# A two-layer decoder trunk: SwiGLU before the weight splits, first units split inside the down loop, transposes behind half a tile, another first chunk

## The chip, the cores and the metric

One core of a Trainium2 chip. The metric is device time in microseconds (us), the median of the runs of the whole program.

## The reference

Two post-norm layers on x of 512 tokens by 1024 features, float32. Each layer has three sub-layers; each sees x scaled and shifted by vectors made from a conditioning vector c.

```python
cond = jax.nn.silu(c)
for l in range(DEPTH):                       # DEPTH = 2
    mod = cond @ w_ada[l] + b_ada[l]         # nine vectors of 1024
    sh1, sc1, g1, sh2, sc2, g2, sh3, sc3, g3 = jnp.split(mod, 9)
    y = _swiglu(x * (1 + sc1) + sh1, ...)    # (silu(h @ w_gate) * (h @ w_up)) @ w_down, D_FF = 2816
    x = layer_norm(ALPHA * x + 0.5 * (1 + g1) * y)
    y = _token_mixer(x * (1 + sc2) + sh2, w_in[l], w_out[l])
    x = layer_norm(ALPHA * x + (1 + g2) * y)
    y = _swiglu(x * (1 + sc3) + sh3, ...)
    x = layer_norm(ALPHA * x + 0.5 * (1 + g3) * y)
```

The token mixer (retention, dilated and stick-breaking heads between two projections) is not touched.

## The kernel before

**Products.** Every weight product is done in three matmuls (`mm3`, L181 to L183): both operands are split into a rounded part `hi` and a remainder `lo`, and hi x hi, hi x lo and lo x hi are added in PSUM. A *unit* is a 128 x 1024 piece of a weight matrix. `unit` (L167) loads it into one of three `raw` buffers, ScalarE casts it to `hi` (L176) and VectorE takes the difference `lo` (L177). `hi` and `lo` go to one of four buffers of their own, or, for a unit marked spare, to two of the 22 large buffers that also hold the hidden tiles. All loads are issued by SyncE in one queue.

**Background.** The modulation vectors of later sub-layers are made meanwhile from 512 KB pieces of w_ada, which pass through the same three `raw` buffers: a load and a multiply-add on VectorE (L205) for each of eight pieces, then a reduction across partitions on GpSimd (L209) and a few operations on VectorE (L216 to L221). `pacer` (L264) spreads these steps evenly over a number of calls. A multiply-add is issued one step after its load.

**A feed-forward** (`ffn`, L445). The 22 hidden tiles (128 features by 512 tokens) come in groups of two, one group last where the number is odd, as in the first feed-forward, where three tiles are made in the start-up. A group takes four units (two for a single tile): gate, then up. When the gate products are done, ScalarE takes silu (L415); when the up products are done, VectorE multiplies (L420), ScalarE casts (L421) and VectorE takes the difference (L422). After each unit the unit four places on is loaded and split (`load(1)`) and the background advances (`next(pace)`). Then the down product: for each of the first 18 hidden tiles i one unit of w_down serves four row tiles of 128 tokens with two PSUM banks each, all eight; it is 24 matmuls (`rows_mm`, L397 to L401). The last four units are kept for a tail that goes row tile by row tile (`rows_tail`), so that the norm of one runs under the products of the next. Between loop and tail, `prefetch()` loads and splits the first four units of the next sub-layer.

**Between two sub-layers** (`PostNorm`, L317). For each row tile: gate, residual and statistics on VectorE (L349 to L354), the root on GpSimd (L146), the scaling on ScalarE (L362). `make_h` transposes normalised tiles for the next sub-layer: 16 transposes for a pair of row tiles (L297), scale and shift on ScalarE and VectorE (L301, L303), cast and difference (L307, L308). The first pair is done in `head()`, after the products of row tile 2 and before those of row tile 3; the second pair in `rest()`, inside the next sub-layer.

**The start-up** (`startup`, L1041) makes the first sub-layer's modulated x in eight chunks of 128 features. `sums(k)` loads the chunk's shift and scale weights and x, multiplies by c on VectorE and GpSimd and adds; `chunk(k)` finishes the sum with a matmul against ones (L1092), transposes x (L1089), and makes `hT_hi` and `hT_lo`; then the three hidden tiles get the chunk's products.

The order on each engine is set by a scheduler from the order of the program and its own estimates of time; `issue_after(ins)` puts what follows behind `ins` on the same engine's queue, without a wait of its own.

Of the kernel before, what the change touches and what calls it, by code (L numbers as in the profile page):

```python
# [67 lines left out]
def trunk(ctx: ExitStack, tc: tile.TileContext, x_in, c_in, w_ada, b_ada, ln_gain, ln_bias,  # L68
# [47 lines left out]
    def load_cols():  # L116
        pt = psum()
        for l in range(DEPTH):
            PE.transpose(out=pt[:, l * NB:(l + 1) * NB], in_=brows[:, l, :], identity=ident[0:NB, 0:NB])
        V.tensor_copy(out=bcol.rearrange("p l c -> p (l c)"), in_=pt[:, 0:DEPTH * NB])  # L120
# [166 lines left out]

    def make_h(pair, h, a, b):
        hh, hl = h
        sl = slice(pair * 256, pair * 256 + 256)  # L290
        for k2 in range(KC // 2):
            ps = psum()
            tmp = work([P, 512], "htmp")
            for i in range(2):
                k = k2 * 2 + i
                for t in range(2):
                    PE.transpose(out=ps[:, i * 256 + t * P:i * 256 + (t + 1) * P],  # L297
                                 in_=xres[pair * 2 + t][:, k * P:(k + 1) * P], identity=ident)
# [18 lines left out]
    class PostNorm:  # L317
# [58 lines left out]

        def head(self):

            if self.h is not None:
                make_h(0, self.h, self.a, self.b)  # L380

# [21 lines left out]
    def rows_part(ps, parts, cs, fresh):  # L403
        for i, ((sh, sl), (wh, wl)) in enumerate(parts):
            mm3(ps, sh, sl, wh[:, cs], wl[:, cs], fresh and i == 0, i == len(parts) - 1)
        return ps
# [6 lines left out]
    def silu(ps_g):  # L413
        sg = work([P, T], "sg")
        S.activation(out=sg, in_=ps_g, func=AF.Silu)  # L415
        return sg

    def glu(sg, ps_u):
        g = big([P, 2, T], F32R, "gT")
        V.tensor_tensor(out=sg, in0=sg, in1=ps_u, op=ALU.mult)  # L420
        S.copy(out=g[:, 0, :], in_=sg)  # L421
# [13 lines left out]
    REST_AT_Q = 3  # L435
    AHEAD = 3
    RES, RES_END = 4, 8
    ACT_HEADS = (1, 3)
# [6 lines left out]
    def ffn(l, s, wg, wu, wd, h, pre, gt, rest, prefetch, nxt):  # L445
# [56 lines left out]
        for i in range(NF - res):  # L502
# [24 lines left out]

    def proj_units(l, off, spare=False):
        return [unit(w_in[l, kh * 512:(kh + 1) * 512, off:off + 256].rearrange("(k p) f -> p k f", p=P), (4, 256), spare)
                for kh in range(2)]  # L530

# [27 lines left out]
    def mixer(l, h, pre, rest, prefetch, nxt):  # L559
# [469 lines left out]
        for k in range(4):  # L1029
            ws(k)  # L1030
        npre = prefetch()
        pn = PostNorm(l, 1, nxt)
# [8 lines left out]
    def startup():  # L1041
# [6 lines left out]
        def sums(k):  # L1048
# [27 lines left out]
            last = V.tensor_tensor(out=accs[0], in0=accs[0], in1=accs[1], op=ALU.add)  # L1076
            with tc.issue_after(last.ins), tc.issue_after(cond_ins.ins):
                uls[k] = unit([(0, f1g[0, cs, 0:384]), (1, f1u[0, cs, 0:384])], (2, 384))
            return accs[0], last

        def chunk(k, acc):
            cs = slice(k * P, (k + 1) * P)
            if k == 0:
                load_cols()
                V.tensor_copy(out=bc0[:, 0, :], in_=mod_bias(0, 0))
                V.tensor_scalar(out=bc0[:, 1, :], in0=mod_bias(0, 1), scalar1=1.0, scalar2=None, op0=ALU.add)
            px = psum()
            for t in range(NT):
                PE.transpose(out=px[:, t * P:(t + 1) * P], in_=xres[t][:, cs], identity=ident)  # L1089
            pc = psum()  # L1090
            for m in range(2):
                PE.matmul(pc[:, m:m + 1], lhsT=acc[:, m, :], rhs=ones[:, 0:1], start=True, stop=True)  # L1092
            ab0 = small([P, 2], "ab0")
            V.tensor_tensor(out=ab0, in0=pc[:, 0:2], in1=bc0[:, :, k], op=ALU.add)
            tmp = work([P, T], "htmp")
            S.activation(out=tmp, in_=px, func=AF.Identity, scale=ab0[:, 1:2], bias=ab0[:, 0:1])
            S.copy(out=hh[:, k, :], in_=tmp)  # L1097
            done = V.tensor_tensor(out=hl[:, k, :], in0=tmp, in1=hh[:, k, :].bitcast(F32), op=ALU.subtract)  # L1098
            return done

        acc, last = sums(0)
        last = chunk(0, acc)
# [15 lines left out]
        load_cols2()  # L1118
        return h, [glu(silu(pss[0][m]), pss[1][m]) for m in range(3)]

# [11 lines left out]
    def first_units(l, s):  # L1132
        if l >= depth:
            return None
        if s == 1:
            return proj_units(l, OFF["sv"], True) + proj_units(l, OFF["sq"], True)
        return [u() for u in gu_loads(l, *((f1g, f1u) if s == 0 else (f2g, f2u)), 0, 2, True)]

# [43 lines left out]
```

## Time and profile before

| | |
|---|---|
| runs | 1986.51 us median of 3 (1985.47 to 1992.09) |
| the profiled execution | 1992.88 us, of which span 1991.1 |
| mean granted TensorE clock | 0.995 |
| TensorE busy with matmuls | 1951.0 us, 98% |
| VectorE, ScalarE, GpSimd busy | 1146.7, 685.3, 234.3 us |
| moved by DMA | 263.12 MB |

The first feed-forward runs from the start to 405 us, the first mixer to about 640, then two feed-forwards with a boundary at 1011.5, the second mixer from 1380, and the last feed-forward to the end. Matmuls overlap, so a TensorE that is busy to 98% isn't at its peak; what counts are the stretches in which it stands still or has a low clock. In a row of an engine's order, the brackets hold how long the engine sat idle before the instruction, and what ended that.

### The profile page before, as it was taken

The page shows a single profiled execution, that of the slowest core. Times are in us where ns is not written, and L with a number is a line of the kernel's source. Part 1 is how long each engine was busy: PE and PEld are TensorE (multiplying, and loading weights), DVE is VectorE, ACT ScalarE, POOL GpSimd, SP SyncE. Part 2 cuts the span into 40 slices and gives each one's busy share as a digit, 9 for nine tenths or more (in the row PEclk, how much of TensorE's full clock was granted, in tenths as well). Part 3 has the DMA queues.
Part 4 walks back from the last instruction along what each step waited for, and adds up shares of the span by engine and source line. Part 5 has one row for each costly group of instructions (what it writes and reads, how often), then busy time and mean ns, then how long its engine had stood idle before and what let it go on. Part 6 is the DMA issues. An engine that isn't in the chain of part 4 may idle for free.

```text
span 1991.1 us, 24802 instructions
## 1 busy us (share of the span) xinstructions
PE 1951.0 (98%) x10008; PEld 1637.6 (82%) x10008; DVE 1146.7 (58%) x1525; ACT 685.3 (34%) x952; POOL 234.3 (12%) x180
## 2 busy tenths in 40 slices
PE   7999979999999999999999999999999999999998
PEld 5888868898888988888888888888887888888887
DVE  8555664556767575664567455436576665434327
ACT  3322221346653323231242233213575442222220
POOL 5011111103210011110101011010133000001000
PEclk9999989999999999999999999999999999999999
DMA  9555555532222445545424444442322223434231
GB/s 291 165 172 177 182 170 166 169 106 80 75 73 75 136 160 172 177 159 177 141 92 156 155 158 159 148 148 85 106 69 83 75 74 106 128 125 138 96 106 53
DMA packets 177930, 263.12 MB, mean 132 GB/s; under 512 B 8602, under 2 KB 144018, under 8 KB 177816
## 3 DMA queue, kind: packets, MB, share of 16 engines
q1 hardware_dynamic: 177816, 261.55, 41.3%
q8 instruction: 78, 1.28, 0.3%
q14 instruction: 36, 0.29, 0.0%
HBM read 259.42 MB, written 2.10 MB: 131 GB/s over the span
## 4 chain that ended last, share of the span: by engine, by line
PE 77%; DVE 7%; DMA 6%; ACT 6%; issue 2%; POOL 1%; SPq 0%; DVEq 0%; ACTq 0%; POOLq 0%
PE ps L181 19%; PE ps L182 19%; PE ps L183 19%; PE ps L397 5%; PE ps L401 5%; PE ps L398 5%; DMA raw<-in_ffn_w_down_dram 3%; DVE lo L177 2%; DMA raw<-in_ffn_w_up_dram 2%; ACT hi L176 2%; ACT rtmp L683 1%; PE ps L297 1%; DMA raw<-in_w_in_dram 1%; DMA raw<-in_ffn_w_gate_dram 1%; PE ps L654 1%
## 5 line engine op out<-in xcount | busy, mean ns | idle before, releaser
L177 DVE TENSOR_TENSOR lo<-raw,hi 128x1024 fp32r<-128x1024 f32 (+1 forms) x298 | 410.6, 1380 | 603.0 <-ACT hi L176 602.3
L176 ACT CAST hi<-raw 128x1024 fp32r<-128x1024 f32 (+1 forms) x298 | 310.8, 1045 | 800.7 <-DMA raw<-in_ffn_w_down_dram 161.8
L181 PE MATMUL ps<-hT_hi,hi 128*128 128x512 f32 x1472 | 574.6, 393 | 4.0 <-ACT hT_hi L1097 4.0
L183 PE MATMUL ps<-hT_hi,lo 128*128 128x512 f32 x1472 | 574.4, 390 | 1.6 <-DVE lo L177 1.6
L182 PE MATMUL ps<-hT_lo,hi 128*128 128x512 f32 x1472 | 574.3, 390 | 0.0
L181 PEld LDWEIGHTS ps<-hT_hi,hi 128*128 128x128 f32 x1472 | 276.4, 188 | 65.1 <-ACT hT_hi L1097 5.6
L183 PEld LDWEIGHTS ps<-hT_hi,lo 128*128 128x128 f32 x1472 | 276.8, 188 | 60.4 <-DVE lo L177 2.7
L182 PEld LDWEIGHTS ps<-hT_lo,hi 128*128 128x128 f32 x1472 | 276.9, 188 | 56.8 <-DVE hT_lo L1098 0.8
L209 POOL PARTITION_ALL_REDUCE red<-acc x16 | 102.3, 6397 | 1023.8 <-DVE acc L205 957.8
L397 PE MATMUL ps<-hi,gT 128*128 128x512 f32 x544 | 213.2, 392 | 8.9 <-DVE sg L420 8.9
L398 PE MATMUL ps<-lo,gT 128*128 128x512 f32 x544 | 212.7, 391 | 0.0
L401 PE MATMUL ps<-hi,gT 128*128 128x512 f32 x544 | 168.5, 391 | 0.0
L205 DVE SCALAR_TENSOR_TENSOR acc<-raw,cond,acc 128x1024 f32<-128x1024 f32 x118 | 150.9, 1279 | 0.4
L397 PEld LDWEIGHTS ps<-hi,gT 128*128 128x128 f32 x544 | 102.8, 189 | 31.0 <-DVE sg L420 9.4
L401 PEld LDWEIGHTS ps<-hi,gT 128*128 128x128 f32 x544 | 102.8, 189 | 21.5
L398 PEld LDWEIGHTS ps<-lo,gT 128*128 128x128 f32 x544 | 102.9, 189 | 21.3
L181 PE MATMUL ps<-hi,hT_hi 128*128 128x256 f32 x320 | 93.7, 293 | 0.0
L182 PE MATMUL ps<-lo,hT_hi 128*128 128x256 f32 x320 | 90.5, 283 | 0.0
L183 PE MATMUL ps<-hi,hT_lo 128*128 128x256 f32 x320 | 90.4, 282 | 0.0
L415 ACT ACTIVATE sg<-ps 128x512 f32<-128x512 f32 x88 | 51.5, 594 | 106.1 <-PE ps L183 105.4
L420 DVE TENSOR_TENSOR sg<-sg,ps 128x512 f32<-128x512 f32 x88 | 58.5, 684 | 43.1 <-PE ps L183 43.0
L421 ACT CAST gT<-sg 128x512 fp32r<-128x512 f32 x88 | 52.0, 617 | 58.0 <-DVE sg L420 57.7
(430 smaller groups left out, 2445.5 us busy)
## 6 DMA issues: line engine op xcount, KB each, us to landing
raw<-in_w_ada_dram SPq DMA_DIRECT2D x128, 512.0 KB
raw<-in_ffn_w_down_dram SPq DMA_DIRECT2D x88, 512.0 KB
raw<-in_ffn_w_gate_dram SPq DMA_DIRECT2D x85, 512.0 KB
raw<-in_ffn_w_up_dram SPq DMA_DIRECT2D x85, 512.0 KB
raw<-in_w_in_dram SPq DMA_DIRECT2D x48, 512.0 KB
ada<-in_w_ada_dram SPq DMA_DIRECT2D x32, 256.0 KB
raw<-in_w_out_dram SPq DMA_DIRECT2D x16, 512.0 KB
bcrow<-in_ln_gain_dram SPq DMA_DIRECT2D x6, 512.0 KB
```

Of the source, the lines that this page charges most:

```text
L176: S.copy(out=hi, in_=raw)
L177: mods["dve"] = V.tensor_tensor(out=lo, in0=raw, in1=hi.bitcast(F32), op=ALU.subtract)
L181: PE.matmul(dst, lhsT=sh, rhs=mh, start=first, stop=False)
L182: PE.matmul(dst, lhsT=sh, rhs=ml, start=False, stop=False)
L183: return PE.matmul(dst, lhsT=sl, rhs=mh, start=False, stop=last)
L205: mods["dve"] = V.scalar_tensor_tensor(out=acc, in0=raw, scalar=cond[:, k:k + 1], in1=acc, op0=ALU.mult, op1=ALU.add)
L209: G.partition_all_reduce(st["red"], st["acc"], P, bass_isa.ReduceOp.add)
L397: PE.matmul(ps2[hf], lhsT=sh, rhs=wh[:, cs], start=first, stop=False)
L398: PE.matmul(ps2[hf], lhsT=sh, rhs=wl[:, cs], start=False, stop=False)
L401: PE.matmul(ps2[hf], lhsT=sl, rhs=wh[:, cs], start=False, stop=last)
L420: V.tensor_tensor(out=sg, in0=sg, in1=ps_u, op=ALU.mult)
L421: S.copy(out=g[:, 0, :], in_=sg)
```

## The change

In four places:

1. In the last group of a feed-forward, no background step runs, and the last two of the units that are split there (in the first feed-forward: both) come behind the last gate times up product and the last silu on their engines. The pacer counts the groups without the last.
2. The first four units of the next sub-layer are loaded and split in iterations 10, 12, 14 and 16 of the down loop, one each, in place of after the loop.
3. In the tail of a feed-forward, `head()` comes after the first half (512 of 1024 columns) of row tile 3's products in place of after row tile 2's. The mixer keeps its order.
4. In the start-up's first chunk, VectorE takes six of the eight modulation weights in a row and TensorE the last two as matmuls with the column of c, the weight unit is traced later, and TensorE gets 24 transposes of the identity ahead of the chunk and 24 behind its sums; their results aren't used.

```diff
@@ make_h @@
-    def make_h(pair, h, a, b):
+    def make_h(pair, h, a, b, behind=None):
...
+                    with tc.issue_after(behind.ins) if behind is not None else nullcontext():
+                        PE.transpose(out=ps[:, i * 256 + t * P:i * 256 + (t + 1) * P],
+                                     in_=xres[pair * 2 + t][:, k * P:(k + 1) * P], identity=ident)
@@ ffn @@
+    EARLY = 10
-        pace = pacer(4 * sum(n for _, n in groups) // 2 + NF - res - AHEAD)
+        pace = pacer(4 * sum(n for _, n in groups[:-1]) // 2 + NF - res - AHEAD)
+        ahead, npre = prefetch(), []
+
+        def ahead_units(n):
+            for _ in range(min(n, len(ahead))):
+                npre.append(ahead.pop(0)())
...
                     if sl.stop == T:
+                        end = gi == len(groups) - 1
                         if ui == len(us) // 2 - 1:
                             sg = [silu(pss[0][m]) for m in range(n)]
                         if ui == len(us) - 1:
                             for m in range(n):
-                                gt.append(glu(sg[m], pss[1][m]))
-                        load(0 if first else 1)
-                        next(pace)
+                                gt.append(glu(sg[m][0], pss[1][m]))
+                        if not end:
+                            load(0 if first else 1)
+                            next(pace)
+                        elif ui == len(us) - 1:
+                            with tc.issue_after(mods["glu"].ins), tc.issue_after(sg[-1][1].ins):
+                                load(2)
+                        elif ui < len(us) - 2:
+                            load(1)
...
             load(1)
             next(pace)
+            if i >= EARLY and i % 2 == 0:
+                ahead_units(1)
         drain(1000)
         load(res - 4)
         ws = take(res)
-        npre = prefetch()
+        ahead_units(len(ahead))
...
-            rows_tail(pss[t], parts)
-            if t == 2:
-                pn.head()
+            rows_part(pss[t][0], parts, slice(0, 512), False)
+            if t == NT - 1:
+                pn.head(mods["pe"])
+            rows_part(pss[t][1], parts, slice(512, 1024), False)
             pn.tile(t, pss[t])
@@ startup, sums(k) @@
+            if k == 0:
+                acc = accs[0]
+                for kk in range(KC - 2):
+                    c, w = cond[:, kk:kk + 1], wts[kk // 4][:, kk % 4]
+                    if kk == 0:
+                        V.tensor_scalar(out=acc, in0=w, scalar1=c, scalar2=None, op0=ALU.mult)
+                    else:
+                        last = V.scalar_tensor_tensor(out=acc, in0=w, scalar=c, in1=acc, op0=ALU.mult, op1=ALU.add)
+                return [(wts[1][:, kk % 4], cond[:, kk:kk + 1]) for kk in (KC - 2, KC - 1)] + [(acc, ones[:, 0:1])], last
...
+        def turn(n, after):
+
+            with tc.issue_after(after.ins):
+                for _ in range(n):
+                    after = PE.transpose(out=pss[1][2][:, 0:P], in_=ident, identity=ident)
+            return after
@@ startup, chunk(k) @@
             if k == 0:
...
+                at = turn(24, mods["pe"])
+                with tc.issue_after(at.ins):
+                    for m in range(2):
+                        for i, (acc, c) in enumerate(parts[:-1]):
+                            at = PE.matmul(pss[1][1][:, 2 * i + m:2 * i + m + 1], lhsT=acc[:, m, :], rhs=c, start=True, stop=True)
...
+            if k == 0:
+                turn(24, at)
...
+            made = V.tensor_tensor(out=ab0, in0=pc[:, 0:2], in1=base, op=ALU.add)
...
+            if k == 0:
+                with tc.issue_after(made.ins), tc.issue_after(cond_ins.ins):
+                    uls[k] = unit([(0, f1g[0, cs, 0:384]), (1, f1u[0, cs, 0:384])], (2, 384))
```

The rest hands these values on: `rows_part`, `glu` and `silu` keep their last instruction in `mods` or return it, and `first_units` returns four functions, each of which loads one unit.

## Rows read from the trace of the kernel before

**Rows 1.** Waits of TensorE, whole span: us in total, times, longest.
```profile
PE ps L397 <- DVE sg L420: 8.9, 1, 8.9
...
PE ps L297 <- ACT xall L362: 4.5, 3, 2.6
```

**Rows 2.** TensorE in order: start, us, instruction, [idle before, what ended it].
```profile
283.43 0.79 PE L397 MATMUL ps<-hi,gT 128*128 128x512 f32 x1 [8.95 <-DVE sg L420]
```

**Rows 3.** VectorE in order, the same columns.
```profile
281.57 1.21 DVE L217 TENSOR_REDUCE adac<-red 128x8 f32<-128x1024 f32 x1
282.70 0.68 DVE L420 TENSOR_TENSOR sg<-sg,ps 128x512 f32<-128x512 f32 x1
```

**Rows 4.** Stretches: length; busy us of PE, PEld, DVE, ACT, POOL; PEclk, DMA, GB/s.
```profile
280.00:290.00 10.00, 6.57 (x17) 5.18 (x18) 6.67 (x9) 2.62 (x3) 0.00 (x0) 0.54 0.66 207
...
4.00:48.00 44.00, 34.30 (x158) 27.68 (x159) 38.05 (x80) 13.84 (x19) 26.37 (x24) 1.00 1.16 307
```

**Rows 5.** The chain that ended last, 207 to 372 us, shares by line.
```profile
by line: DMA raw<-in_ffn_w_down_dram 33.9%; DVE lo L177 14.3%; ACT hi L176 12.8%; DMA raw<-in_ffn_w_up_dram 10.4%; DVE acc L205 6.3%; issue 5.3%; DMA raw<-in_ffn_w_gate_dram 4.8%; POOL red L209 4.2%; DMA raw<-in_w_in_dram 3.3%; DMA raw<-in_
```

**Rows 6.** The `raw` buffers, 207 to 372 us: count, ns, first and last; idle.
```profile
L176 ACT CAST hi<-raw x30: 1044/1052/1058, 207.8 to 369.1; 128x1024 fp32r<-128x1024 f32 x30
...
L197 SPq DMA_DIRECT2D raw<-in_w_ada_dram x23: 327/328/382, 213.4 to 348.9; - x23
...
  PE ps L183: 5.1, 1
```

**Rows 7.** SyncE's issues of loads in order, 353 to 372 us.
```profile
353.70 8.68 SPq L175 DMA_DIRECT2D raw<-in_ffn_w_down_dram  x5
362.43 0.42 SPq L314 DMA_DIRECT2D bcrow<-in_ln_gain_dram  x1
368.02 0.33 SPq L314 DMA_DIRECT2D bcrow<-in_ln_bias_dram  x1
368.44 2.10 SPq L175 DMA_DIRECT2D raw<-in_ffn_w_down_dram  x2
371.47 0.38 SPq L175 DMA_DIRECT2D raw<-in_w_in_dram  x1
```

**Rows 8.** The sixteenth down unit: its difference on VectorE, its and the next's start.
```profile
358.42 1.23 DVE L177 TENSOR_TENSOR lo<-raw,hi 128x1024 fp32r<-128x1024 f32 x1 [3.56 <-ACT hi L176]
...
363.33 0.39 PE L397 MATMUL ps<-hi,gT 128*128 128x512 f32 x1
...
368.77 0.39 PE L397 MATMUL ps<-hi,gT 128*128 128x512 f32 x1
```

**Rows 9.** Boundary before the second mixer, VectorE and TensorE in order.
```profile
1361.27 1.23 DVE L177 TENSOR_TENSOR lo__10257<-raw,hi__10256 128x1024 fp32r<-128x1024 f32 x1 [1.31 <-ACT hi__10256 L176]
...
1368.77 0.38 PE L297 MATMUL ps<-ident,xall 128*128 128x128 f32 x2
1371.70 1.54 PE L297 MATMUL ps<-ident,xall 128*128 128x128 f32 x6 [2.55 <-ACT xall L362]
...
1379.50 0.68 DVE L308 TENSOR_TENSOR hT_lo<-htmp,hT_hi 128x512 fp32r<-128x512 f32 x1
...
1380.35 0.28 PE L181 MATMUL ps<-hi__10238,hT_hi 128*128 128x256 f32 x1
```

**Rows 10.** Boundary before the first mixer, TensorE in order.
```profile
396.20 0.38 PE L297 MATMUL ps<-ident,xall 128*128 128x128 f32 x2
397.68 0.77 PE L297 MATMUL ps<-ident,xall 128*128 128x128 f32 x5 [1.10 <-ACT xall L362]
...
405.00 0.28 PE L181 MATMUL ps<-hi__2666,hT_hi 128*128 128x256 f32 x1
```

**Rows 11.** The start-up, TensorE and GpSimd in order.
```profile
11.07 1.01 PE L1092 MATMUL ps<-ones,acc 128*128 128x1 f32 x4 [1.25 <-DVE acc L1076]
...
13.98 1.65 PE L181 MATMUL ps<-hT_hi,hi 128*128 128x512 f32 x3 [1.89 <-ACT hT_hi L1097]
...
45.31 0.93 POOL L1068 TENSOR_SCALAR acc<-ada,cond 128x256 f32<-128x256 f32 x1 [2.36 <-DMA ada<-in_w_ada_dram]
```

More of the change, by code (lines that the diff above doesn't have):

```diff
@@ L1 @@
 import math
-from contextlib import ExitStack
+from contextlib import ExitStack, nullcontext
 import numpy as np
@@ L118, in load_cols @@
         for l in range(DEPTH):
-            PE.transpose(out=pt[:, l * NB:(l + 1) * NB], in_=brows[:, l, :], identity=ident[0:NB, 0:NB])
+            mods["pe"] = PE.transpose(out=pt[:, l * NB:(l + 1) * NB], in_=brows[:, l, :], identity=ident[0:NB, 0:NB])
         V.tensor_copy(out=bcol.rearrange("p l c -> p (l c)"), in_=pt[:, 0:DEPTH * NB])
@@ L296, in make_h @@
                 for t in range(2):
-                    PE.transpose(out=ps[:, i * 256 + t * P:i * 256 + (t + 1) * P],
-                                 in_=xres[pair * 2 + t][:, k * P:(k + 1) * P], identity=ident)
+                    with tc.issue_after(behind.ins) if behind is not None else nullcontext():
+                        PE.transpose(out=ps[:, i * 256 + t * P:i * 256 + (t + 1) * P],
+                                     in_=xres[pair * 2 + t][:, k * P:(k + 1) * P], identity=ident)
                 cs = slice(i * 256, i * 256 + 256)
@@ L375, in finish, with head @@
                 nc.sync.dma_start(out=out[t * P:(t + 1) * P, cs], in_=x[:, cs])
-        def head(self):
+        def head(self, behind=None):
             if self.h is not None:
-                make_h(0, self.h, self.a, self.b)
+                make_h(0, self.h, self.a, self.b, behind)
         def rest(self):
@@ L404, in rows_part @@
         for i, ((sh, sl), (wh, wl)) in enumerate(parts):
-            mm3(ps, sh, sl, wh[:, cs], wl[:, cs], fresh and i == 0, i == len(parts) - 1)
+            mods["pe"] = mm3(ps, sh, sl, wh[:, cs], wl[:, cs], fresh and i == 0, i == len(parts) - 1)
         return ps
@@ L414, in silu @@
         sg = work([P, T], "sg")
-        S.activation(out=sg, in_=ps_g, func=AF.Silu)
-        return sg
+        return sg, S.activation(out=sg, in_=ps_g, func=AF.Silu)
     def glu(sg, ps_u):
         g = big([P, 2, T], F32R, "gT")
-        V.tensor_tensor(out=sg, in0=sg, in1=ps_u, op=ALU.mult)
+        mods["glu"] = V.tensor_tensor(out=sg, in0=sg, in1=ps_u, op=ALU.mult)
         S.copy(out=g[:, 0, :], in_=sg)
@@ L526, in trunk, with proj_loads, proj_units @@
     OFF = dict(rq=0, rk=256, rv=512, rg=1024, dq=1536, dk=1792, dv=2048, sq=2304, sk=2560, sv=2816)
-    def proj_units(l, off, spare=False):
-        return [unit(w_in[l, kh * 512:(kh + 1) * 512, off:off + 256].rearrange("(k p) f -> p k f", p=P), (4, 256), spare)
-                for kh in range(2)]
+    def proj_loads(l, off, spare=False):
+        return [lambda kh=kh: unit(w_in[l, kh * 512:(kh + 1) * 512, off:off + 256].rearrange("(k p) f -> p k f", p=P),
+                                   (4, 256), spare) for kh in range(2)]
+    def proj_units(l, off):
+        return [u() for u in proj_loads(l, off)]
     def hsl(a):
@@ L1030, in mixer @@
             ws(k)
-        npre = prefetch()
+        npre = [u() for u in prefetch()]
         pn = PostNorm(l, 1, nxt)
@@ L1076, in sums @@
             last = V.tensor_tensor(out=accs[0], in0=accs[0], in1=accs[1], op=ALU.add)
-            with tc.issue_after(last.ins), tc.issue_after(cond_ins.ins):
+            with tc.issue_after(last.ins), tc.issue_after(mods["cast"].ins):
                 uls[k] = unit([(0, f1g[0, cs, 0:384]), (1, f1u[0, cs, 0:384])], (2, 384))
-            return accs[0], last
-        def chunk(k, acc):
+            return [(accs[0], ones[:, 0:1])], last
+        def turn(n, after):
[3 more added lines that the diff above has]
+            return after
@@ L1082, in chunk @@
+        def chunk(k, parts):
             cs = slice(k * P, (k + 1) * P)
+            px = psum()
+            pc = psum()
             if k == 0:
[L1084 to L1087, printed above, removed]
+                at = turn(24, mods["pe"])
[3 more added lines that the diff above has]
+                            at = PE.matmul(pss[1][1][:, 2 * i + m:2 * i + m + 1], lhsT=acc[:, m, :], rhs=c, start=True, stop=True)
@@ L1088, in chunk @@
             for t in range(NT):
-                PE.transpose(out=px[:, t * P:(t + 1) * P], in_=xres[t][:, cs], identity=ident)
-            pc = psum()
+                tr = PE.transpose(out=px[:, t * P:(t + 1) * P], in_=xres[t][:, cs], identity=ident)
+            acc, c = parts[-1]
             for m in range(2):
-                PE.matmul(pc[:, m:m + 1], lhsT=acc[:, m, :], rhs=ones[:, 0:1], start=True, stop=True)
+                at = PE.matmul(pc[:, m:m + 1], lhsT=acc[:, m, :], rhs=c, start=True, stop=True)
@@ L1093, in chunk @@
+            if k == 0:
+                turn(24, at)
             ab0 = small([P, 2], "ab0")
-            V.tensor_tensor(out=ab0, in0=pc[:, 0:2], in1=bc0[:, :, k], op=ALU.add)
+            base = bc0[:, :, k]
+            for i in range(len(parts) - 1):
+                V.tensor_tensor(out=ab0, in0=pss[1][1][:, 2 * i:2 * i + 2], in1=base, op=ALU.add)
+                base = ab0
+            made = V.tensor_tensor(out=ab0, in0=pc[:, 0:2], in1=base, op=ALU.add)
             tmp = work([P, T], "htmp")
@@ L1096, in chunk @@
             S.activation(out=tmp, in_=px, func=AF.Identity, scale=ab0[:, 1:2], bias=ab0[:, 0:1])
-            S.copy(out=hh[:, k, :], in_=tmp)
+            if k == 0:
+                with tc.issue_after(made.ins), tc.issue_after(cond_ins.ins):
+                    uls[k] = unit([(0, f1g[0, cs, 0:384]), (1, f1u[0, cs, 0:384])], (2, 384))
+            mods["cast"] = S.copy(out=hh[:, k, :], in_=tmp)
             done = V.tensor_tensor(out=hl[:, k, :], in0=tmp, in1=hh[:, k, :].bitcast(F32), op=ALU.subtract)
@@ L1099, in chunk @@
             return done
+        load_cols()
+        V.tensor_copy(out=bc0[:, 0, :], in_=mod_bias(0, 0))
+        V.tensor_scalar(out=bc0[:, 1, :], in0=mod_bias(0, 1), scalar1=1.0, scalar2=None, op0=ALU.add)
         acc, last = sums(0)
@@ L1118, in startup @@
         load_cols2()
-        return h, [glu(silu(pss[0][m]), pss[1][m]) for m in range(3)]
+        return h, [glu(silu(pss[0][m])[0], pss[1][m]) for m in range(3)]
     def vectors(l, s):
@@ L1133, in first_units @@
         if l >= depth:
-            return None
+            return []
         if s == 1:
-            return proj_units(l, OFF["sv"], True) + proj_units(l, OFF["sq"], True)
-        return [u() for u in gu_loads(l, *((f1g, f1u) if s == 0 else (f2g, f2u)), 0, 2, True)]
+            return proj_loads(l, OFF["sv"], True) + proj_loads(l, OFF["sq"], True)
+        return gu_loads(l, *((f1g, f1u) if s == 0 else (f2g, f2u)), 0, 2, True)
     h, gt = startup()
```

## Prediction

> **What bounds the kernel now.** I read who TensorE waited for first, then the stretches around the longest waits, and last the chain of work that ended last, to see which of these waits cost anything. TensorE waits little in all; two entries concern this change [rows 1]. The longest single wait, 8.95 us up to 283.43, comes in the first SwiGLU feed-forward, at the start of its down product: the eighth PSUM bank is still held by the last hidden tile, whose gate times up product (L420) VectorE starts only at 282.70, behind a vector reduction (L217) and other work that was queued ahead of it [rows 2, 3]. After the wait TensorE runs at half clock (0.54 granted between 280 and 290, so largely the 1.2 GHz level): 6.57 us of work there hold 17 matmuls [rows 4]. A unit of weights is 24 matmuls and takes 5.44 us at the full clock (363.33 to 368.77) [rows 8], 0.227 each; 17 of them would need 3.9, so 2.7 are lost. Wait and clock together: 11.7 us.
>
> The chain of waits says what that is worth. From 207 to 372 us it runs through weight loads, ScalarE's `hi` cast, VectorE's `lo` difference and vector sums [rows 5]. It holds no TensorE work worth a share. So in this stretch the stream of weights and modulation vectors through the three `raw` buffers sets the pace, and a TensorE that stands still loses only what it would have had in hand. I call that stream the ring. It moved 30 weight units and 23 vector loads between 207 and 371.5 [rows 6]: 3.1 us a load. When the vector loads are over it is faster: 353.70 to 371.47 holds eight unit loads and two `bcrow` loads [rows 7], 17.8 / 10 = 1.78 us each.
>
> The other entry is the transposes of the first row pair at a stage's end, 4.5 us in three places, the longest 2.55 [rows 1, 9]. There VectorE is held by the split of the next stage's weights (at 1361.27, after 1.31 us of waiting for its cast), so the normalised tile comes late [rows 9].
>
> **The change part by part.**
>
> *SwiGLU ahead.* In the last group of hidden tiles the two weight units that were split between its products now come behind its silu and its gate times up product, and no vector step runs there. What delayed L420 is gone, and with it up to 11.7 us of TensorE standing or at half clock. What the ring allows: the sixteenth down unit was ready at 358.42 + 1.23 = 359.65 and TensorE began it at 363.33 [rows 8]. If TensorE came 11.7 earlier, it would wait there for 8.0 of them. So the part is worth 3.7 if the ring keeps its times, and 11.7 if it does not bind. The chain bears the first out. The two units that now wait hold two `raw` buffers until TensorE has done the last up product; behind them in the queues of ScalarE and VectorE stand the casts and differences of later units, which TensorE wants over 20 us later (four units of 5.44), so this costs nothing there.
>
> Does the ring change? The vector steps of the first feed-forward are the same (six vectors, 48 loads, 69 steps), spread over 51 calls in place of 53, so each unit has 1.353 in place of 1.302. By the sixteenth down unit both kernels have done the same number (63.6 and 63.8 steps). But one load more (28 units x 0.051 x 48/69) is done by 207 us, where a cast waited 5.1 us for TensorE [rows 6], so there was room for it. The ring then has one load less to carry: between 0 and 3.1, I take 2.0, as that wait is longer than the load.
>
> *First units split during down.* Four units (a 512 KB load, a cast of 1.05, a difference of 1.23 [rows 6, 8]) move from behind the down loop into its iterations 10, 12, 14 and 16. Engine time is no issue: ScalarE casts one or two units in 5.44 us, VectorE has one or two differences and 1.35 vector sums. They take the scarce thing, `raw` buffers and a place in SyncE's queue, ahead of the last weights and of the `bcrow` loads. One comes before the sixteenth unit: between 1.78 and 3.1 us, I take 2.5, because the last vector loads run just there. That leaves 3.7 + 2.0 - 2.5 = 3.2 at the sixteenth unit, so it starts at 360.1. After it the ring has six weight units, three first units and two `bcrow` loads to bring: 11 x 1.78 = 19.6, to 379.7. TensorE reaches the tail three units later, 376.4, and needs its fourth unit nine matmuls on, 378.5. It waits 1.2. First feed-forward: 3.2 - 1.2 = 2.0 gained. In the other feed-forwards I cost the move at nothing: their stream has no place on the chain; if it had, each unit would cost the same 1.78 to 3.1.
>
> *Transposes behind half of the last tile's products.* Removed: three waits of 2.55, 1.10 and 0.85 (the rest of 4.5) [rows 1, 9, 10]. The longest also costs clock. From the first transpose to the next stage's first product it took 405.00 - 396.20 = 8.80 at the first boundary, 7.70 without its wait [rows 10], and 1380.35 - 1368.77 = 11.58 at the other [rows 9]: 3.9 lost. Together 5.8. The transposes now come twelve matmuls, 2.72 us, later, and VectorE no longer splits there: the tile that was ready at 1371.70 [rows 9] would now be needed at 1368.77 + 2.72 = 1371.49 and come earlier by the waiting split, so no wait remains. What is late next: the casts behind the transposes. They took from 1371.70 to 1379.50 + 0.68 = 1380.2 [rows 9], 8.5 us, of which some 1.4 are half clock (six transposes take 1.54 us there, five 0.77 at 397.68 [rows 9, 10]). Now they end 2.72 + 7.1 = 9.8 after the point at which the next stage would start 7.70 later; that stage needs its last quarter after six of eight steps of three 0.12 us matmuls, at 7.70 + 2.16 = 9.86. There is no margin. I take 0.3 lost at each of the two mixers, where a step is that short: 5.8 - 0.6 = 5.2. Bounds: 5.8, and 0 if all of it comes back as a wait for these casts. Queued behind such a wait are only the next stage's products.
>
> *First chunk.* Eight modulation weights were multiplied on VectorE and GpSimd; now VectorE takes six in a row and TensorE two, and 48 dummy transposes run, 24 before and 24 behind. The product with the sums, at 11.07, waited 1.25 us for VectorE, and the first three matmuls on the chunk, from 13.98, take 1.65 us [rows 11], where at full clock 0.39 + 2 x 0.227 = 0.84 would do: the clock is low there. Up to 1.25 us sooner and at full clock, TensorE would be some 3 us ahead when the second chunk comes. But the start-up is bound elsewhere: 307 GB/s without a break from 4 to 48 us [rows 4], and the last chunk's sums begin when their weights land, at 45.31 [rows 11]. The order of loads is the same, so nearly all of the lead becomes waiting. Between 0 and 1.3; I take 0.7, half. If the dummies do not raise the clock, the 24 behind the sums, at six in 1.54 us [rows 9], take 6 us where there are 13.98 - 11.07 = 2.9 now, and hold the first chunk back by 3; 0 to 3 of that reach the end, half of it 1.5. The Trainium skill (TensorE: Matmul & The Clock Gate, Part 4: PE-mode transpose) states that transposes do not count as activity for the clock. No row of this kernel shows a long run of transposes alone, and by that rule the sum would be 7.9 - 0.7 - 1.5 = 5.7 in place of 7.9.
>
> **The sum.** 2.0 + 5.2 + 0.7 = 7.9 us. The profiled execution took 1992.88 (span 1991.1 and 1.8 around it): 1985.0. It lies 6.4 above the median of the runs, 1986.51; the gain is in places that every run has, so for the median 1978.6.
>
> **The rivals.**
> - *The ring does not bind.* With the last group free of vector steps, the splits gain what TensorE gains. 11.7 + 5.2 + 0.7 = 17.6: 1968.9. For it: the wait is the longest of all. Against it: the chain has no TensorE work for 164 us [rows 5]. The Trainium skill (Perfetto Trace Analysis, Optimization Strategy) would look for the gaps of the most contended engine and remove them; by that the gap's full 11.7 would count.
> - *The wait at the boundary only moves* to the casts (no margin, above): 2.0 + 0.7, 1983.8.
> - *The dummies do not raise the clock*: 0.7 is not gained and 1.5 lost: 1980.8. Nothing in the rows speaks for or against it: at half clock TensorE is doing matmuls and transposes alike.
> - *The first units starve the down loop* (the other side). If each takes its turn in a chain of one buffer, load, cast, difference, load, its price is the 5.95 us from the load at 353.70 to the end of its difference at 359.65 [rows 7, 8]: 3.7 + 2.0 - 23.8 = -18.1, and with 5.9 gained elsewhere 1998.7. It decides from 4.4 us a unit on: 0.7 + 5.2 + 3.7 + 2.0 - 4 x 4.4 = -6.0. For it: the buffers are the scarce thing. Against it: 1.78 a load where no vectors run.
>
> **How the numbers follow.** About 0.3%, 6 us, is what can be told from no change. Chances: forecast 0.40 (its own range 1973 to 1983), ring not binding 0.20, wait moves 0.18, dummies 0.10, starving 0.12. Faster: most of the first (0.34), all of the second, 0.04 of the dummies: 0.58. Slower: 0.12 less a part that stays under 4.4 a unit, 0.11. The same: 0.31. The range takes in all but the starving case and the tip of the second: 1967 to 1988.
>
> **What would show it.** The wait of L397 for L420 gone or under 1 us; new waits of down matmuls (L397, L398, L182) for `hi` and `lo` of the first feed-forward, a few us in all, near its end and in its tail; the waits of L297 for L362 gone; waits of the next stage's L181 for `hT` under 1 us each; the clock full before 13 us. Wrong, if weights never hold TensorE up in the first feed-forward (then 1969), or if they do for over 10 us.

## The result, and the profile after

The changed kernel takes 1999.11 us (median, 1996.99 to 2001.14), the kernel before 1987.44 in the same runs: a ratio of 1.006, 95% interval 1.0049 to 1.0071, 11.7 us slower. I had forecast 1978.6 and at most 1988. The profiled execution has a span of 1999.2 us, 8.1 more than that of before; as the profiled execution of before lies 5.4 above its median and that of the changed kernel 1.9, the two traces show less than the 11.7.

Who TensorE waited for, in the changed kernel's whole span (us in total, times, longest):

```profile
PE ps L183 <- DVE lo L177: 6.1, 6, 3.3
PE ps L181 <- ACT hi L176: 4.5, 3, 3.9
PE ps L398 <- ACT hi L176: 3.0, 2, 1.6
PE ps L298 <- ACT htmp L302: 2.4, 3, 0.8
...
PE ps L398 <- DVE sg L420: 1.6, 1, 1.6
PE ps L399 <- DVE lo L177: 1.5, 2, 0.8
```

Both waits that the change aimed at have gone or shrunk: 8.9 us for the product to 1.6, and the transposes no longer wait for the normalised tile [rows 1]. In their place TensorE waits for the `hi` and `lo` of weights, 15 us over the lines L181, L183, L398 and L399, where before it had 1.6 (0.39 and 1.24 us at 257 and 264 us).

The changed kernel by stretch (busy us of each engine and instructions, granted clock PEclk, DMA):

```profile
core 0: us, PE busy (x) PEld busy (x) DVE busy (x) ACT busy (x) POOL busy (x), PEclk, DMA share, GB/s
60.00:210.00 150.00, 148.16 (x648) 121.09 (x648) 85.08 (x83) 41.00 (x53) 14.95 (x3) 1.00 0.53 170
210.00:265.00 55.00, 51.29 (x217) 41.32 (x216) 34.41 (x34) 14.88 (x19) 7.97 (x2) 0.97 0.53 169
265.00:295.00 30.00, 27.17 (x116) 21.22 (x116) 17.61 (x19) 8.57 (x10) 2.35 (x1) 1.00 0.50 159
295.00:350.00 55.00, 55.00 (x245) 45.55 (x244) 24.97 (x26) 9.46 (x9) 7.99 (x2) 1.00 0.53 172
350.00:410.00 60.00, 50.97 (x203) 40.07 (x202) 36.47 (x41) 14.67 (x14) 7.26 (x3) 0.91 0.44 149
```

The loss has two places: before the down loop (190 to 265 us), and its end with the tail (350 to 410, where the clock fell to 0.91). The second pair's transposes, which close a boundary, start at 425.56 (before: 413.63), 1031.32 (1020.18) and 1397.12 (1388.99). So the first feed-forward loses 11.9 us and the two later boundaries give back 0.8 and 3.0. Up to the tail's first product (385.07, before 379.65) the 5.4 us split so: start-up -1.0; waits 12.75 against 10.58, +2.2; the rest, +4.3, is TensorE slower behind its waits: from 214.66 to 217.22 and from 368.41 to 370.97 its 128x512 matmuls take 0.63 us in place of 0.39. (From the first silu, at 57.40 and 58.41, to the tail, less the waits, it took 314.9 us and 310.7; a kernel below without waits takes 306.9.)

The longest wait before the loop (start, duration, engine, instruction, idle before it):

```profile
207.80 6.41 POOL L209 PARTITION_ALL_REDUCE red<-acc  x1 [44.34 <-DVE acc L205]
...
209.44 4.27 DVE L177 TENSOR_TENSOR lo<-raw,hi 128x1024 fp32r<-128x1024 f32 x1 [0.61 <-ACT hi L176]
...
213.77 0.51 PE L183 MATMUL ps<-hT_hi,lo 128*128 128x512 f32 x1 [3.29 <-DVE lo L177]
```

The weight's cast ended at 209.42, and its difference, 1.23 us elsewhere, took 4.27 beside GpSimd's reduction; with 1.23 it would have ended at 210.67, 0.2 us after TensorE's last product (an estimate from these rows). The wait of 1.24 us at 266.91 follows such a difference too (5.33 us from 261.52), so 4.5 of the 6.7 us of waits for weights ahead of the down loop come where a reduction meets a weight without lead. The kernel before has the same meeting: its wait at 264.53 follows a difference that took 5.53. No kernel here moves the reductions, so their own share of the loss is not measured. And in the tail:

```profile
388.45 1.04 ACT L176 CAST hi__2703<-raw 128x1024 fp32r<-128x1024 f32 x1 [5.30 <-DMA raw<-in_w_in_dram]
389.40 1.99 ACT L176 CAST hi<-raw 128x1024 fp32r<-128x1024 f32 x2
```

`hi__2703` is a first unit of the mixer. The last two down units are cast behind it; TensorE waited 3.90 us for the first of them, to 390.49.

### The profile page after: what moved, and what is told of

Same layout as the page of the kernel before. It is cut to its first block, busy times and chain, and to the rows that moved or that the text cites. A ratio compares the mean times of both kernels' runs of the same rounds, so it can differ in the third digit from the quotient of the medians.

```text
span 1999.2 us, 24912 instructions
## 1 busy us (share of the span) xinstructions
PE 1960.6 (98%) x10064; PEld 1642.2 (82%) x10064; DVE 1145.0 (57%) x1525; ACT 684.6 (34%) x952; POOL 230.0 (12%) x177
## 4 chain that ended last, share of the span: by engine, by line
PE 79%; DVE 7%; ACT 5%; DMA 5%; issue 2%; POOL 1%; SPq 1%; DVEq 0%; ACTq 0%; POOLq 0%
PE ps L181 20%; PE ps L182 19%; PE ps L183 19%; PE ps L398 6%; PE ps L399 6%; PE ps L402 6%; DVE lo L177 2%; DMA raw<-in_ffn_w_down_dram 2%; ACT rtmp L702 1%; ACT hi L176 1%; DMA raw<-in_ffn_w_up_dram 1%; PE ps L298 1%; DMA ada<-in_w_ada_dram 1%; DMA raw<-in_w_in_dram 1%; PE ps L673 1%
## 5 line engine op out<-in xcount | busy, mean ns | idle before, releaser
L177 DVE TENSOR_TENSOR lo<-raw,hi 128x1024 fp32r<-128x1024 f32 (+1 forms) x298 | 403.4, 1356 | 575.9 <-ACT hi L176 569.4
L183 PE MATMUL ps<-hT_hi,lo 128*128 128x512 f32 x1472 | 575.4, 391 | 6.2 <-DVE lo L177 6.1
L176 ACT CAST hi<-raw 128x1024 fp32r<-128x1024 f32 (+1 forms) x298 | 310.7, 1045 | 789.0 <-DMA raw<-in_ffn_w_up_dram 200.1
L181 PE MATMUL ps<-hT_hi,hi 128*128 128x512 f32 x1472 | 575.7, 393 | 1.0 <-ACT hi L176 0.6
L183 PEld LDWEIGHTS ps<-hT_hi,lo 128*128 128x128 f32 x1472 | 276.7, 188 | 66.4 <-DVE lo L177 9.2
L181 PEld LDWEIGHTS ps<-hT_hi,hi 128*128 128x128 f32 x1472 | 276.7, 188 | 62.1 <-issue 2.5
L398 PE MATMUL ps<-hi,gT 128*128 128x512 f32 x544 | 212.9, 391 | 4.5 <-ACT hi L176 3.0
L399 PE MATMUL ps<-lo,gT 128*128 128x512 f32 x544 | 212.6, 391 | 1.5 <-DVE lo L177 1.5
L398 PEld LDWEIGHTS ps<-hi,gT 128*128 128x128 f32 x544 | 102.5, 189 | 27.8 <-ACT hi L176 3.8
L399 PEld LDWEIGHTS ps<-lo,gT 128*128 128x128 f32 x544 | 102.5, 188 | 23.3 <-DVE lo L177 2.1
L181 PE MATMUL ps<-hi,hT_hi 128*128 128x256 f32 x320 | 93.8, 293 | 0.0
L183 PE MATMUL ps<-hi,hT_lo 128*128 128x256 f32 x320 | 90.5, 283 | 0.0
```

The lines of the kernel that those rows point to most:

```text
L176: S.copy(out=hi, in_=raw)
L177: mods["dve"] = V.tensor_tensor(out=lo, in0=raw, in1=hi.bitcast(F32), op=ALU.subtract)
L181: PE.matmul(dst, lhsT=sh, rhs=mh, start=first, stop=False)
L183: return PE.matmul(dst, lhsT=sl, rhs=mh, start=False, stop=last)
L398: PE.matmul(ps2[hf], lhsT=sh, rhs=wh[:, cs], start=first, stop=False)
L399: PE.matmul(ps2[hf], lhsT=sh, rhs=wl[:, cs], start=False, stop=False)
```

## The experiments

Ratios are to the kernel before on the same chip, whose medians there were 1988.07 us (first four kernels), 1991.30, 1991.04 and 1992.28 (last three). 0.0010 is 2.0 us, and a difference in us is worked out from the ratios unless two medians stand beside it.

**Which part did it.** Theory A, from the two traces: the first units, in the raw buffers ahead of the last weights. Theory B: the SwiGLU part. I undid or did one part at a time; the diffs of single parts are those of the change.

`late_first`: the changed kernel with

```diff
-    EARLY = 10
+    EARLY = 100
```

> The changed kernel with its four first units put back behind the down loop; the other three parts stay. Theory A (the four units take turns in the three raw buffers ahead of the last down weights of the first feed-forward, and this is where the time went; the other parts give 1 us at the start, about 4 us at the boundaries and nothing at the SwiGLU): about 5 us under the kernel before, 0.9975, with no wait of a matmul for hi or lo over 1 us between 340 and 400 us. Theory B (the SwiGLU part did it: the vector steps that come denser before the down loop use up TensorE's lead, which shows as its 5.0 us of waits for lo between 190 and 214 us, and the two units held behind the product delay the rest; the first units are harmless): 5 us or more over the kernel before, 1.0025 or higher, and the waits between 340 and 400 us stay.

`only_first`, `only_glu`, `only_half`: the kernel before with part 2, part 1 or part 3.

> The kernel before with one part alone: the next stage's four first units issued in iterations 10, 12, 14 and 16 of the down loop. Theory A: 11 to 13 us over the kernel before, 1.006, with waits for hi and lo in the last down units and in the tail of the first feed-forward of 8 us or more. Theory B: within 2 us of the kernel before.

> The kernel before with the SwiGLU part alone. Theory A: the 8.95 us wait goes and the ring gives nothing, so within 2 us of the kernel before, and the waits for lo between 190 and 214 us of about 5 us are there too, since the denser vector steps are. Theory B: 5 to 8 us over the kernel before. The prediction had 3.7 + 2.0 = 5.7 under it.

> The kernel before with one part alone: the first pair's transposes behind half of the last tile's products. Theory A: the waits of the transposes for the normalised tile (2.55, 1.10, 0.85 us) go and 4 to 5 us are gained, 0.9977. Rival: the wait only moves to the casts behind the transposes and the time is within 1 us of the kernel before.

| kernel | median us | ratio | 95% interval |
|---|---|---|---|
| late_first | 1994.82 | 1.0033 | 1.0021 to 1.0045 |
| only_first | 1990.54 | 1.0012 | 1.0004 to 1.0021 |
| only_glu | 1993.72 | 1.0034 | 1.0022 to 1.0045 |
| only_half | 1986.30 | 0.9996 | 0.9987 to 1.0004 |

Theory A falls. Theory B holds for the SwiGLU part, not in full: the first units alone cost 2.4 us (0.8 to 4.2), just over its 2, and without them (`late_first`) the waits for weights between 340 and 400 us, which it expected to stay, fall from 9.0 us to 2.6. TensorE's waits in `only_first`, 60 to 425 us:

```profile
PE ps L398 <- DVE sg L420: 7.7, 1, 7.7
PE ps L181 <- ACT hi L176: 3.6, 1, 3.6
PE ps L182 <- DVE lo L177: 0.7, 1, 0.7
```

The last two are in the tail; the first is the old wait. The SwiGLU part alone costs 6.8. No single trace shows where: that of `only_glu` reaches the tail at 375.58, that of `only_half`, which has the old code up to there, at 375.56, and that of before at 379.65, so one execution of a kernel differs from another by as much. On top of the others the first units cost 0.0027 (1.0033 to 1.006), 5.4 us, against 2.4 alone; the intervals of the two prices overlap. The transposes gain nothing that can be told from no change. Where their wait went is seen in `only_half` at the third boundary (order of the engines, some lines):

```profile
1367.34 1.04 PE L298 MATMUL ps<-ident,xall 128*128 128x128 f32 x8
...
1369.56 0.16 DVE L362 SCALAR_TENSOR_TENSOR nmr<-mv,rstd 128x1 f32<-128x1 f32 x1 [0.66 <-POOL rstd L146]
...
1369.76 1.24 ACT L363 ACTIVATE xall<-xall,nmr,rstd 128x1024 f32<-128x1024 f32 x1 [2.73 <-DVE nmr L362]
...
1370.91 1.46 ACT L302 ACTIVATE htmp<-ps,b_col,a_col 128x256 f32<-128x256 f32 x3
...
1371.51 0.44 PE L298 MATMUL ps<-ident,xall 128*128 128x128 f32 x2 [2.20 <-ACT htmp L302]
```

Eight of the sixteen transposes run on time. The ninth waits 2.20 us for a PSUM bank that `htmp` (L302) must empty. `htmp` stands on ScalarE behind the scaling of row tile 2 (L363), which waits for that tile's statistics: `head()` now comes after `tile(2)` in the program; before, it came ahead of it. At the three boundaries together TensorE waits 4.2 us for these banks, against the 4.5 for the tile that the part removed.

**Which half of the SwiGLU part.** On `only_glu`, either the old pace with the held units, or the new pace without them:

```diff
@@ glu_hold: pacer counts all groups; in the last group
+                        next(pace)
@@ glu_rate: pacer counts groups[:-1]; loads as before
+                        load(0 if first else 1)
+                        if not end:
+                            next(pace)
```

> Half of the SwiGLU part on the kernel before: the two weight units of the last group come behind the silu and the product, but the vector steps are paced as in the kernel before, in the last group too. Theory C (the raw buffers set the pace; the part lost because the buffers stand idle while the two units are held, and because the denser vector steps make each earlier weight later; about half each): about 3 us over the kernel before, 1.0015. Theory D (the denser steps alone did it): within 1.5 us of the kernel before. Theory E (the held units alone did it): 6 us over, 1.003.

> The other half on the kernel before: no vector steps in the last group, so the same steps over 51 calls in place of 53, but the two weight units stay where they were, split between the products. Theory C: about 3 us over the kernel before, 1.0015, with waits for hi and lo of some 3 us between 190 and 215 us. Theory D: 6 us over, 1.003. Theory E: within 1.5 us of the kernel before, or faster by up to 4 us if the wait for the product goes too.

`glu_hold` 1992.34 us, 1.0007 (0.9998 to 1.0016). `glu_rate` 2002.26 us, 1.0048 (1.0034 to 1.0062). So it is the pace, as theory D had it: two calls fewer for the same vector steps. TensorE's waits in `glu_rate`, 60 to 425 us:

```profile
PE ps L398 <- DVE sg L420: 6.5, 2, 5.7
PE ps L183 <- DVE lo L177: 6.1, 7, 2.4
PE ps L181 <- ACT hi L176: 2.1, 2, 1.5
```

8.2 us for weights, all before the down loop, and the wait for the product is still there. To see whether the place of the loads does it, I kept the old number and pace and moved them all one step ahead:

```diff
-    def pacer(units):
+    def pacer(units, owed=0.0):
...
-        rate, owed = len(bg) / units, 0.0
+        rate = len(bg) / units
...
+ NF - res - AHEAD, 1.0 if (l, s) == (0, 0) else 0.0)
```

> The kernel before, in which the pacer of the first feed-forward starts with one step owed, so every vector load there stands one step earlier among the weight loads; their number and the rate are the same. Theory C (a vector load set ahead of a weight costs the weight one load's time, about 3 us, where TensorE has no lead left, and half clock behind the stall): 3 to 8 us over the kernel before, 1.0015 to 1.004, with waits for hi and lo of 3 us or more before the down loop. Rival (the place of the loads does not matter, only their number, and the paced part lost by what it does in the last group): within 1.5 us.

`one_early`: 1998.41 us, 1.0033 (1.0020 to 1.0045), 6.6 us, with 7.6 us of waits for weights before the loop:

```profile
PE ps L397 <- DVE sg L420: 5.3, 1, 5.3
PE ps L181 <- ACT hi L176: 3.9, 3, 1.9
PE ps L183 <- DVE lo L177: 3.7, 6, 1.3
```

Setting each vector load one place ahead, with their number and rate as before, is enough; 1.3 of the 7.6 us follow a difference stretched by a reduction.

**Whether the raw buffers are the reason.** A fourth buffer, paid for with one large tile; and the control with the tile alone gone.

```diff
-    bigp = ctx.enter_context(tc.tile_pool(name="bigp", bufs=22))
-    rawp = ctx.enter_context(tc.tile_pool(name="rawp", bufs=3))
+    bigp = ctx.enter_context(tc.tile_pool(name="bigp", bufs=21))
+    rawp = ctx.enter_context(tc.tile_pool(name="rawp", bufs=4))
```

> The kernel before with four raw buffers in place of three, and 21 in place of 22 large tiles to make room. Theory C: two loads then take less than the 5.9 us they take now, TensorE is ahead of the weights in the whole first feed-forward, no matmul waits for hi or lo of a weight there, and the time falls by 3 us or more unless the missing large tile holds something up. Rival (the number of buffers is not what sets the pace; the loads take as long as the transfers or VectorE need): 15 to 20 loads less than 1 us nearer, the pace stays 5.9 us for two loads and the time within 1.5 us of the kernel before.

> The changed kernel with four raw buffers and 21 large tiles. Theory C: the waits for hi and lo in the first feed-forward (about 20 us in all in the changed kernel) go, and it falls by 10 us or more, to the level of the kernel before with four buffers or below it. Rival: it stays within 3 us of the changed kernel, 1.006 of the kernel before.

> The kernel before with 21 in place of 22 large tiles and three raw buffers: the control for the kernels with four. If the fourth raw buffer gave the 20 us there: within 1.5 us of the kernel before. Rival (the missing large tile holds later work back and so changes the order for the better): 5 us or more under it.

`before_raw4` 1970.58 us, 0.9895 (0.9881 to 0.9908). `after_raw4` 1973.02, 0.9907 (0.9894 to 0.9921). `before_big21` 1989.85, 0.9997 (0.9988 to 1.0006). The buffer is worth 20.7 us in the kernel before; in the changed one the ratio goes from 1.006 to 0.9907, about 30 by the ratios. What ended ScalarE's idle time ahead of its weight casts, 60 to 400 us, shows it: first the kernel before, then `before_raw4`:

```profile
L176 ACT CAST hi<-raw 128x1024 fp32r<-128x1024 f32 x58 | 61.0, 1051 | 205.3 <-DMA raw<-in_ffn_w_down_dram 82.7 <-DMA raw<-in_ffn_w_gate_dram 52.3 <-DMA raw<-in_ffn_w_up_dram 51.0
```

```profile
L176 ACT CAST hi<-raw 128x1024 fp32r<-128x1024 f32 x57 | 60.1, 1054 | 181.2 <-PE ps L182 78.2 <-PE ps L401 55.8 <-DMA raw<-in_ffn_w_up_dram 19.0
```

With three buffers the casts wait for loads, 186 of 205 us: the weights come just in time, whatever TensorE does. With four, 134 of 181 us are waits for TensorE to free a weight buffer: it is the weights that have the lead. TensorE then waits for nothing in the first feed-forward, not even for the product (`before_raw4`):

```profile
60.00:210.00 150.00, 150.00 (x663) 124.13 (x662) 94.31 (x88) 44.90 (x58) 18.36 (x3) 1.00 0.60 183
210.00:265.00 55.00, 55.00 (x244) 45.56 (x243) 36.08 (x40) 16.11 (x21) 6.12 (x1) 1.00 0.61 192
265.00:295.00 30.00, 30.00 (x134) 24.82 (x133) 17.97 (x16) 6.27 (x7) 7.01 (x2) 1.00 0.60 193
```

By the traces 15.9 of the 22.6 us between the spans of before and `before_raw4` are gained by the second pair's transposes of the first boundary (413.63 to 397.74), 2.1 more by the second (1020.18 to 1002.16) and 4.0 by the third (1388.99 to 1366.94).

**The parts with four buffers.** There the runs of one kernel lie within 1.7 us, and each part's own price can be read.

> The start-up part alone, on the kernel with four raw buffers and 21 large tiles, where single executions differ little. That kernel measured 0.9895 of the kernel before. The profiled start-up with the part reaches the first silu 0.8 us sooner than without: 0.8 us under it, 0.9891. Rival: the lead becomes waiting and nothing is left, 0.9895 or above.

> The part with the transposes behind half of the last tile's products alone, on the kernel with four raw buffers. There no transpose waits for its tile without the part, so nothing can be gained: the transposes wait 0.8 us for the casts behind them at each boundary, and the boundaries take some 1.0 us longer each: 3 us over that kernel, 0.991. Rival: within 1 us of it, 0.9895.

> The SwiGLU part alone, whole, on the kernel with four raw buffers. With three it cost 0.0034. Theory C (it cost that because the denser vector steps met a TensorE without any lead): 0.0 to 0.5 us from the kernel with four buffers, 0.9895, with no wait for a weight and none for the product. Rival (the part costs by itself, by its held units or its silu): 3 us or more above it, 0.991.

> The first units issued during the down loop, alone, on the kernel with four raw buffers. With three it cost 0.0012, by 4.2 us of waits in the tail. Theory C: no wait in the tail, and the time within 0.5 us of the kernel with four buffers, 0.9895. Rival (VectorE and ScalarE have no room for the splits in the loop): 2 us or more above it.

> The start-up part without its 48 dummy transposes, on the kernel with four raw buffers. With them 0.9891. If the dummies raise TensorE's clock (the matmuls behind them take 0.18 us in place of 0.40 between 14 and 16 us): the first products take the long time again, 0.40 us each before 18 us, but as the start-up is bound by its loads the end moves by less than 0.5 us. Rival, the rule that transposes do not raise the clock: the pace of the first products is the same with and without, and leaving the dummies out gains up to 1 us.

| part on before_raw4 | median us | ratio | 95% interval |
|---|---|---|---|
| none | 1970.58 | 0.9895 | 0.9881 to 0.9908 |
| start-up | 1969.64 | 0.9891 | 0.9876 to 0.9906 |
| start-up without dummies | 1970.05 | 0.9887 | 0.9873 to 0.9902 |
| half of the tile | 1973.99 | 0.9912 | 0.9898 to 0.9925 |
| SwiGLU | 1970.83 | 0.9893 | 0.9878 to 0.9907 |
| first units | 1970.25 | 0.9889 | 0.9872 to 0.9905 |

The intervals are as wide as the spread of the kernel before makes them; the medians differ by less. SwiGLU and first units cost nothing that can be told where the weights have a lead. The transposes cost 3.4, which is why `after_raw4` stays 2.4 above `before_raw4`. In the trace of `half_raw4` the three second pairs start 1.77, 2.68 and 3.69 us later than in `before_raw4` (399.51, 1004.84, 1370.63 against 397.74, 1002.16, 1366.94). Of that 0.78 are there when the tail begins (365.83 against 365.05) and are no work of the part: the first silu already starts 0.81 later (58.97 against 58.16), with the same start-up. So 0.9 to 1.0 are lost at each boundary, 2.9 in all. Their wait for the bank remains, now without any gain against it (`half_raw4`, first boundary):

```profile
385.08 1.03 PE L298 MATMUL ps<-ident,xall 128*128 128x128 f32 x8
...
386.07 1.25 ACT L363 ACTIVATE xall<-xall,nmr,rstd 128x1024 f32<-128x1024 f32 x1 [4.26 <-DVE nmr L362]
...
387.22 1.46 ACT L302 ACTIVATE htmp<-ps,b_col,a_col 128x256 f32<-128x256 f32 x3
...
387.81 0.44 PE L298 MATMUL ps<-ident,xall 128*128 128x128 f32 x2 [0.77 <-ACT htmp L302]
```

The start-up's first products, 13 to 20 us, with the dummies and then without (busy us, mean ns of one):

```profile
L181 PE MATMUL ps<-hT_hi,hi 128*128 128x512 f32 x6 | 2.5, 424 | 0.0
```

```profile
L181 PE MATMUL ps<-hT_hi,hi 128*128 128x512 f32 x4 | 2.1, 673 | 1.7 <-ACT hT_hi L1137 1.7
```

The dummies do make TensorE faster there (between 14 and 16 us it begins twelve matmuls against five). They speed up themselves as well: the 24 ahead of the chunk take 5.33 us from 3.46, the 24 behind its sums 2.82 from 10.40. But the loads swallow the lead: the first silu starts at 57.20 with them, 57.54 without, 58.16 with the old start-up. Over all traces it starts at 57.20 to 57.67 with the new start-up (five) and at 57.58 to 59.13 with the old (twelve), so the 0.9 of the part is shown in the mean alone, and the dummies' own part of it isn't shown. No kernel beats `before_raw4` by more than can be told; it and its variants beat both kernels by about 1%.

## Why the prediction was wrong, step by step

- **SwiGLU ahead, forecast 5.7 us gained (3.7 + 2.0); measured 6.8 lost.** The step that failed is the second: "one load more ... is done by 207 us, where a cast waited 5.1 us for TensorE, so there was room for it. The ring then has one load less to carry". The mechanism, the three buffers setting the pace, was right, and I drew the wrong sign from it. If the loads set the pace, a weight behind one more vector load is late by about one load, 3.1 us by my own figure, wherever TensorE has less lead than that. The 5.1 us was one row; at 257 and 264 us TensorE already waited. `one_early` prices this at 6.6 us, `glu_rate` at 9.5; the intervals overlap. That the load is missing later, for which I counted 2.0, shows as no gain in any run.
- **The 3.7 for the wait itself** didn't come either: `glu_hold`, the half of the part that holds the units, is not told apart from no change. The wait is a symptom: with four buffers it is gone with the old code.
- **First units, forecast 3.7 lost (2.5 + 1.2), in an overall gain of 2.0 for the first feed-forward.** Alone they lost 2.4; behind the SwiGLU part 5.4. That the second price is higher because the lead that I had counted (3.7 at the sixteenth unit) was used up is argued from the waits, as the intervals overlap. My 1.78 us a load was too small by its own rows: ten issues between 353.70 and 371.47 make nine steps, 1.97 each, and the wait in the tail becomes 3.3 in place of 1.2 [rows 7]; `only_first` waited 4.3 there. The place was right, four waits between 357 and 367 us and the tail. So was the bracket: the rival that starves the down loop, at 5.95 us a unit, had this mechanism, but no unit was that dear, and alone the part costs less than I took. That its time, 1998.7, is near the measured one comes from other terms.
- **Transposes, forecast 5.2; measured 0.8 with -0.8 to 2.6 as its interval.** The failed step is "no wait remains". I asked when the tile and the casts would be ready and missed the order on ScalarE: `head()` moved past `tile(2)`, so its casts queue behind a scaling that waits for statistics, and half of the transposes wait for their banks. The rival in which the wait moves to the casts was the true case; it stands on the transposes rather than on the next stage's products. Between the boundaries of the first and second feed-forward the changed kernel gave 0.8 back, between those of the second and third 3.0.
- **First chunk, forecast 0.7; measured 0.9** (1970.58 to 1969.64), in keeping with the mechanism given, a lead that the loads swallow; the ratios, 0.9895 and 0.9891, don't tell it from nothing. The dummies raise the pace, so the rival fell. The rule of the Trainium skill (TensorE: Matmul & The Clock Gate, Part 4: PE-mode transpose), that transposes don't count as activity, is not what this trace shows, 424 ns against 673 behind them, and 0.22 us each in the first 24 dummies against 0.12 in the second; the granted clock reads 1.00 from 14 to 16 us in both, so the profile's clock column doesn't show it.
- **"Wrong ... if they do for over 10 us"** was the sign that came true: 15 us of waits for weights, and 4.3 us more of slow products behind them.
- **Still open:** whether the parts together lose more than one by one: 11.7 us (9.7 to 14.1) against about 7.5 (6.8 + 2.4 - 0.8 - 0.9), a sum whose terms are each uncertain by about 2; how much of the loss the reductions on GpSimd add; and whether more than four buffers would bring more, which was not tried.

## What to carry to other kernels

Before moving work in a stream that is loaded, cast and used, read what ends the idle time of its middle step: if it is the load, the consumer has no lead, and what is put ahead is paid for in waits (here 6.6 us for one place); if it is the consumer, there is room. A long wait inside such a stretch may be a symptom of the stream, so try one buffer more before reordering around it. When a block of operations is moved, look at its place in every engine's queue, not only at when its inputs are ready.

## What the runs showed of the hardware that I had not expected

- VectorE's difference of a weight takes 1.23 us, and 4.27 when it starts while GpSimd's partition all-reduce runs (209.44, above). It ended at 213.71, 0.50 us before the reduction's recorded end at 214.21. So it is in all 17 kernels: of the 253 differences that start more than 1.7 us before the recorded end of an all-reduce, 252 end 0.50 to 0.52 us before that end, whenever they started, and take 1.26 to 5.61 us; the 71 that start later take 1.21 to 1.23. With four raw buffers the same stretch costs TensorE nothing (5.25 us at 197.51 in `before_raw4`). The Trainium skill (SBUF — State Buffer, SBUF: two separate sides) has a port pair that the two share and lock for a whole instruction. The rows agree that the reduction holds VectorE up, but VectorE finishes before the reduction's recorded end, so not for the whole of the recorded instruction; the recorded spans of GpSimd are rough.
- Runs of the kernel before reach from 1985.3 to 1994.8 us (23 of them in one group from 1985.3 to 1991.2), those of the five kernels with four raw buffers and the old boundary from 1969.4 to 1972.1. The spread goes with the late weights: that the time of the loads is what varies is argued from that, not shown.
